# Linear ReLU attention on one core: the last stores cut into 120 and 8 partitions, the first four stores ungated

## The chip, the cores and the metric

One core of a Trainium2 chip runs the kernel. The time is device time in microseconds (us), as the median of several executions. A profile is one execution; its span, from the first to the last instruction, is about 1.8 us shorter than that execution's time.

## The reference

For each of 8 x 12 heads with 512 tokens of 64 numbers, fp32:

```python
Q_feat, K_feat = np.maximum(0, Q), np.maximum(0, K)
KV = np.einsum('bhkd,bhkv->bhdv', K_feat, V)
K_sum = np.sum(K_feat, axis=2)
numerator = np.einsum('bhqd,bhdv->bhqv', Q_feat, KV)
denominator = np.einsum('bhqd,bhd->bhq', Q_feat, K_sum)
return numerator / (denominator[:, :, :, None] + 1e-10)
```

It reads 37.75 MB and writes 12.58 MB, with little arithmetic: the transfers are the work.

## The kernel before

24 groups of four heads. A tile of a group has 128 partitions, each with 16 tokens (4 KB of fp32 in a row of memory). GpSimd issues the loads (they cast to bf16), SyncE the stores. The parts that matter here:

```python
def prep(g): ...      # relu and mask of K, copy of V          (VectorE)
def mm_kv(g):         # 32 small matmuls a group               (TensorE)
    for r in range(R):
        for t in range(2):
            nc.tensor.matmul(ps_kv[g][:, t, 0:D1], kf[g][ts_, r, :, :]..., vo[g % NB][ts_, r, :],
                             start=(r == 0), stop=(r == R - 1), skip_group_check=True)
# ... transposes of Q, output matmuls, normalisation into o_sb ...

def store(g, o_sb):
    if g + DELAY < NG and g % 2 == 0:      # the gate: wait until K of group g + 8 has landed
        nc.sync.dma_start(out=scratch, in_=k_sb[g + DELAY][0:1, 0, :])
    parts = 2 if g >= NG - 4 else 1
    n = R // parts
    for j in range(parts):
        rs = slice(n * j, n * (j + 1))
        nc.sync.dma_start(out=Or[g].rearrange("p (r d) -> p r d", d=D)[:, rs], in_=o_sb[:, rs])

for g in range(NG):   # cut to its order
    mm_kv(g); ...; prep(g + 1); mm_out(g - 1); store(g - 1, norm(g - 1)); transp(g); ...
```

The gate is a load of 128 bytes out of the K tile of eight groups later. SyncE works in order, so it holds back the stores behind it, in favour of the loads. Each transfer has a semaphore, a counter; the trace has 16 raises of it for a transfer that runs on 16 engines, and these are the landing times below.

Of the kernel before, what the change touches and what calls it, by code (L numbers as in the profile page):

```python
# [10 lines left out]
def kernel(  # L11
# [7 lines left out]
    nc = tc.nc  # L19
    B, H, S, D = Q.shape  # L20
    assert D == 64
    P = 128
# [4 lines left out]
    R = S * NHG // P  # L27
    U = R // 2
    NG = NH // NHG
    assert NG * NHG == NH and R == 16  # L30
    DELAY = 8
# [22 lines left out]
    def rview(X):  # L54
        return X.rearrange("b h s d -> (b h s d)").rearrange("(n p f) -> n p f", p=P, f=R * D)

    Qr, Kr, Vr, Or = rview(Q), rview(K), rview(V), rview(out)
# [116 lines left out]



    def store(g, o_sb):
        if g + DELAY < NG and g % 2 == 0:
            nc.sync.dma_start(out=scratch, in_=k_sb[g + DELAY][0:1, 0, :])
        parts = 2 if g >= NG - 4 else 1  # L180
        n = R // parts
        for j in range(parts):
            rs = slice(n * j, n * (j + 1))
            nc.sync.dma_start(out=Or[g].rearrange("p (r d) -> p r d", d=D)[:, rs], in_=o_sb[:, rs])

    zero(0)
    prep(0)
    for g in range(NG):
        mm_kv(g)
        evac_kv(g)  # L190
        if g + 1 < NG:
            if g + 1 < NB:
                zero(g + 1)
            prep(g + 1)
        if g > 0:
            mm_out(g - 1)
            store(g - 1, norm(g - 1))
        transp(g)
        evac_qt(g)
    mm_out(NG - 1)  # L200
    store(NG - 1, norm(NG - 1))


# [28 lines left out]
```

## Time and profile before

| | before |
|---|---|
| time | 130.03 us (129.72 to 130.11, 3 runs) |
| span of the profile | 128.1 us |
| busiest compute engine | DVE, 63% of the span |
| share of the 16 DMA engines | 90% or more in 38 of 40 slices |
| last compute / last store landed | 121.2 us / 126.95 us |

The prediction shows the page's rows. Here is what it doesn't show, the stores and gates in the list of DMA issues of the kernel before. The columns are the tiles, the issuing queue, the count, the size of each and the median us from issue to landing:

```profile
out_dram<-o_sb SPq DMA_DIRECT2D x20, 512.0 KB, 8.8
out_dram<-o_sb SPq DMA_DIRECT2D x8, 256.0 KB, 7.2
scratch<-k_sb SPq DMA_DIRECT2D x8, 0.1 KB, 4.7
```

A store takes 7 to 9 us to land though it moves 0.5 MB: it stands in full queues.

### The profile page before, as it was taken

The numbers are of one execution on the slowest core, as the hardware profiler recorded it, in microseconds if no ns is written. First come the engines' busy times: TensorE is split into PE (matmuls) and PEld (weight loads), VectorE is DVE, ScalarE is ACT, GpSimd is POOL, SyncE is SP. The second block draws the span as 40 slices with busy tenths as digits, with TensorE's granted clock in tenths as the row PEclk, the third lists the DMA queues.
The fourth block names the chain that finished last, engine by engine and source line by source line (L and its number), as shares of the span: only waits on it lengthen the run. The fifth ranks groups of instructions, "written<-read, shape, count | busy, mean of one in ns | idle before, by whom it ended". The sixth has DMA issues, their size and how long they took to land.

```text
span 128.1 us, 4127 instructions
## 1 busy us (share of the span) xinstructions
PE 73.7 (58%) x1728; PEld 54.9 (43%) x1728; DVE 80.3 (63%) x230; ACT 51.0 (40%) x121; POOL 39.4 (31%) x74
## 2 busy tenths in 40 slices
PE   0037864878957818728746855583781874566100
PEld 0036643556644616526535634362460653354100
DVE  1258886798887557748728738456753872886600
ACT  4024774366464433633633452433453363326000
POOL 6905445354535133224133313323331400000000
PEclk9999998555595555555555555555555558757855
DMA  3999999999999999999999999999999999999991
GB/s 109 380 299 212 208 211 209 211 210 209 210 209 260 303 223 241 305 236 232 305 246 211 310 264 211 291 283 209 235 307 242 228 311 246 230 386 411 404 362 67
DMA packets 14673, 32.76 MB, mean 256 GB/s; under 512 B 1856, under 2 KB 1856, under 8 KB 14656
## 3 DMA queue, kind: packets, MB, share of 16 engines
q0 software_dynamic: 9792, 17.83, 74.6%
q1 hardware_dynamic: 4576, 13.63, 28.1%
q10 hardware_dynamic: 288, 1.05, 2.1%
q8 instruction: 13, 0.21, 0.6%
q14 instruction: 4, 0.03, 0.1%
HBM read 37.75 MB, written 12.58 MB: 393 GB/s over the span
## 4 chain that ended last, share of the span: by engine, by line
DMA 79%; POOL 4%; PE 3%; DVE 3%; issue 3%; ACT 2%; POOLq 0%; ACTq 0%
DMA q_sb<-in_Q_dram 41%; DMA v_sb<-in_V_dram 30%; DMA k_sb<-in_K_dram 8%; DVE o_sb L168 2%; ACT qt L143 2%; PE ps_qt L139 1%; POOL q_sb L82 1%; POOL v_sb L78 1%; PE ps_out L154 1%; PE ps_kv L124 1%; POOL k_sb L76 1%; DVE vo L116 1%; DVE rec L167 1%; DVE den L165 0%; POOL ident masks.py:199 0%
## 5 line engine op out<-in xcount | busy, mean ns | idle before, releaser
L124 PE MATMUL ps_kv<-vo,kf 64*128 64x65 bf16 x768 | 24.1, 233 | 32.8 <-DVE vo L116 32.3
L133 ACT CAST kvd<-ps_kv 64x130 bf16<-64x130 f32 x96 | 25.3, 263 | 32.4 <-PE ps_kv L124 30.5
L143 ACT ACTIVATE qt<-ps_qt 128x1024 bf16<-128x1024 bf16 x24 | 24.6, 1024 | 33.4 <-PE ps_qt L139 33.4
L124 PEld LDWEIGHTS <-kf 64*128 64x128 bf16 x768 | 20.5, 122 | 38.3 <-DVE vo L116 30.3
L168 DVE TENSOR_TENSOR o_sb<-ps_out,rec 128x512 f32<-128x512 f32 x48 | 33.2, 691 | 1.7
L154 PE MATMUL ps_out<-kvd,qt 128*32 128x130 bf16 x768 | 28.0, 295 | 10.6 <-DVE o_sb L168 6.5
L114 DVE TENSOR_SCALAR kf<-k_sb,mask 128x1024 bf16<-128x1024 bf16 x44 | 19.4, 483 | 19.3 <-DMA k_sb<-in_K_dram 19.1
L154 PEld LDWEIGHTS <-qt 128*32 128x32 bf16 x768 | 16.9, 123 | 19.3 <-DVE o_sb L168 12.0
L139 PE MATMUL ps_qt<-ident,q_sb 128*128 128x128 bf16 x192 | 23.3, 298 | 2.1 <-DMA q_sb<-in_Q_dram 2.1
L82 POOL DMA_DIRECT2D q_sb<-in_Q_dram x24 | 15.4, 641 | 19.7 <-DMA k_sb<-in_K_dram 16.8
L139 PEld LDWEIGHTS <-q_sb 128*128 128x128 bf16 x192 | 17.4, 135 | 6.6 <-issue 3.8
L78 POOL DMA_DIRECT2D v_sb<-in_V_dram x22 | 11.7, 530 | 25.1 <-DMA q_sb<-in_Q_dram 20.4
L76 POOL DMA_DIRECT2D k_sb<-in_K_dram x22 | 11.9, 541 | 17.8 <-DVE den L165 6.5
L116 DVE COPY vo<-v_sb 128x1024 bf16<-128x1024 bf16 x22 | 9.5, 430 | 10.0 <-DMA v_sb<-in_V_dram 10.0
L167 DVE RECIPROCAL rec<-den 128x8 f32<-128x8 f32 x48 | 9.7, 203 | 1.7
L165 DVE TENSOR_SCALAR den<-ps_out 128x8 f32<-128x8 f32 x48 | 7.5, 156 | 2.0 <-PE ps_out L154 2.0
L114 DVE TENSOR_SCALAR kf<-k_first,mask 128x1024 bf16<-128x1024 f32 x4 | 2.8, 750 | 5.3 <-DMA k_first<-in_K_dram 5.3
L133 ACT ACT_TABLE_LOAD x1 | 1.3, 1283 | 1.7 <-DVE kvd L107 1.7
L116 DVE CAST vo<-v_first 128x1024 bf16<-128x1024 f32 x2 | 1.4, 694 | 0.0
L105 DVE MEMSET mask<- 32x1 f32 x8 | 0.3, 59 | 0.9 <-PEq L216 0.8
L107 DVE MEMSET kvd<- 128x260 f32 x3 | 0.8, 275 | 0.0
masks.py:199 POOL TENSOR_SCALAR_AFFINE_SELECT ident<-ident 128x128 bf16<-128x128 bf16 x1 | 0.3, 287 | 0.1
(6 smaller groups left out, 0.8 us busy)
## 6 DMA issues: line engine op xcount, KB each, us to landing
out_dram<-o_sb SPq DMA_DIRECT2D x20, 512.0 KB, 8.8
q_sb<-in_Q_dram POOLq DMA_DIRECT2D x24, 256.0 KB, 12.5
k_sb<-in_K_dram POOLq DMA_DIRECT2D x22, 256.0 KB, 12.5
v_sb<-in_V_dram POOLq DMA_DIRECT2D x22, 256.0 KB, 12.4
out_dram<-o_sb SPq DMA_DIRECT2D x8, 256.0 KB, 7.2
v_first<-in_V_dram ACTq DMA_DIRECT2D x2, 512.0 KB, 6.7
k_first<-in_K_dram SPq DMA_DIRECT2D x2, 512.0 KB, 6.4
scratch<-k_sb SPq DMA_DIRECT2D x8, 0.1 KB, 4.7
```

The lines of the kernel that those rows point to most:

```text
L76: nc.gpsimd.dma_start(out=k_sb[g].rearrange("p r d -> p (r d)"), in_=Kr[g])
L78: nc.gpsimd.dma_start(out=v_sb[g].rearrange("p r d -> p (r d)"), in_=Vr[g])
L82: nc.gpsimd.dma_start(out=q_sb[g].rearrange("p u f -> p (u f)"), in_=Qr[g])
L114: nc.vector.tensor_scalar(kf[g][:, :, s, :], k_sb[g], scalar1=0.0, scalar2=mask[:, s:s + 1], op0=Alu.max, op1=Alu.mult)
L116: nc.vector.tensor_copy(vo[g % NB][:, :, 0:D], v_sb[g])
L124: nc.tensor.matmul(ps_kv[g][:, t, 0:D1], kf[g][ts_, r, :, :].rearrange("p s d -> p (s d)"), vo[g % NB][ts_, r, :], start=(r == 0), stop=(r ...
L133: nc.scalar.copy(kvd[g % NB][64 * c:64 * c + 64, :, s, c, :], ps_kv[g][64 * s:64 * s + 64, :, 0:D1])
L139: nc.tensor.transpose(ps_qt[g][:, u, :], q_sb[g][:, u, :], ident)
L143: nc.scalar.activation(qt[g].rearrange("p u q -> p (u q)"), ps_qt[g].rearrange("p u q -> p (u q)"), Act.Relu)
L154: nc.tensor.matmul(po[hs, v // 2, (v % 2) * 2 * D1:(v % 2) * 2 * D1 + 2 * D1], qt[g][:, u, hs], kvd[g % NB][:, h // 2, h % 2, :, :], start ...
L167: nc.vector.reciprocal(rec, den)
L168: nc.vector.tensor_tensor(o_sb[:, 8 * j:8 * j + 8].rearrange("p (b r) d -> p b r d", b=2), pv[:, :, :, 0:D], rec.unsqueeze(3).to_broadcast ...
```

## The change

Its intent: one of the 16 DMA engines, number 15, is held to be behind at the end; so the last stores give it nothing. 120 partitions run on the other 15 engines, and the 8 partitions left on the first eight. (This is the rule under (1) in the prediction. Wherever an engine is named below, its number comes from that rule.) With it, the gates of groups 0 and 2 go, and groups 20 and 21 are stored whole.

```diff
     def store(g, o_sb):
-        if g + DELAY < NG and g % 2 == 0:
+        if 4 <= g < NG - DELAY and g % 2 == 0:
             nc.sync.dma_start(out=scratch, in_=k_sb[g + DELAY][0:1, 0, :])
-        parts = 2 if g >= NG - 4 else 1
-        n = R // parts
-        for j in range(parts):
+        last = g >= NG - 2
+        n = R // 2 if last else R
+        for j in range(R // n):
             rs = slice(n * j, n * (j + 1))
-            nc.sync.dma_start(out=Or[g].rearrange("p (r d) -> p r d", d=D)[:, rs], in_=o_sb[:, rs])
+            for ps in (slice(0, 120), slice(120, P)) if last else (slice(0, P),):
+                nc.sync.dma_start(out=Or[g].rearrange("p (r d) -> p r d", d=D)[ps, rs], in_=o_sb[ps, rs])
```

## The prediction

> **What bounds the kernel now.** I read the page first: the DMA row, the chain, the queues; then the waits of SyncE, the busy time by windows, and the landing times that the trace keeps.
>
> ```profile
> DMA  3999999999999999999999999999999999999991
> GB/s 109 380 299 212 208 211 209 211 210 209 210 209 260 303 223 241 305 236 232 305 246 211 310 264 211 291 283 209 235 307 242 228 311 246 230 386 411 404 362 67
> ...
> q0 software_dynamic: 9792, 17.83, 74.6%
> q1 hardware_dynamic: 4576, 13.63, 28.1%
> ...
> q8 instruction: 13, 0.21, 0.6%
> ...
> HBM read 37.75 MB, written 12.58 MB: 393 GB/s over the span
> ...
> DMA 79%; POOL 4%; PE 3%; DVE 3%; issue 3%; ACT 2%; POOLq 0%; ACTq 0%
> ```
>
> The DMA row is 9 in 38 of 40 slices: the transfer engines are full from 3 us to about 124 us, while the busiest compute engine is DVE with 63%. GB/s counts what lands: a load reads fp32 and lands bf16, so 210 there is 420 read. Load stretches (420), mixed stretches and the stores at the end (404 to 411) all move about the same HBM traffic. A store that goes earlier or later only changes the order of work in full queues. What can change the time is idle time at the two ends.
>
> ```profile
> 122.00:124.00 2.00, 0.00 (x0) 0.00 (x0) 0.00 (x0) 0.00 (x0) 0.00 (x0) 0.50 1.04 400
> 124.00:125.00 1.00, 0.00 (x0) 0.00 (x0) 0.00 (x0) 0.00 (x0) 0.00 (x0) 0.50 0.63 244
> 125.00:126.00 1.00, 0.00 (x0) 0.00 (x0) 0.00 (x0) 0.00 (x0) 0.00 (x0) 0.50 0.38 145
> 126.00:127.00 1.00, 0.00 (x0) 0.00 (x0) 0.00 (x0) 0.00 (x0) 0.00 (x0) 0.50 0.11 43
> ```
>
> The last two columns are the DMA engines' share and their GB/s. All compute is over at 121.19 us (end of the last o_sb multiply). Until 124 the engines are full with stores, then they run dry one after the other: a ragged end. The trace keeps 16 landing times for every transfer, one for each DMA engine, without the engine's name. For the last store, after the first at 124.20 us, they come at +0.04, 0.07, 0.31, 0.40, 0.44, 0.79, 0.94, 1.00, 1.41, 1.57, 2.18, 2.52, 2.53, 2.68 and 2.75 us (126.95). Their mean is +1.23. So the whole ragged end is worth at most 2.75 - 1.23 = 1.5 us, 1.2% of the time, even if every engine ended at once. The span ends 1.1 us after the last landing.
>
> ```profile
> SPq L179 <- DMA k_sb<-in_K_dram: 72.3, 8, 33.9
> SPq L179 <- DMA scratch<-k_sb: 20.4, 7, 3.4
> SPq L184 <- DMA out_dram<-o_sb: 6.6, 6, 2.0
> ```
>
> The first line is the gate of the stores: before every even group up to 14, SyncE waits until K of eight groups later has landed (35.5 us for the first, then every 10.2 us). The third matters for the end: a store waits for an older store. The semaphores in the trace show why: SyncE's transfers go round eight semaphores, so each issue waits until the transfer eight before it has landed on all 16 engines. The last six stores were issued at 115.24, 116.86, 118.18, 119.41, 120.64 and 121.85 us, each about 0.06 us after such a landing.
>
> **What the Trainium skill says.** (1) "DMA: Bandwidth & Descriptors", section "Why a DMA increments its semaphore by 16 and not by 1": the number of engines of a transfer is the largest k up to 16 that divides the outer dimension, and on the sync queue these are the lowest-numbered k. So 120 partitions go to engines 0 to 14 with 8 each, and 8 partitions to engines 0 to 7 with one each; engine 15 gets none of the last two groups. The trace before has only transfers cut 16 ways, so it can't test this. (2) Same page, "Latency and other measured facts": engines 7 and 15 are usually slower than the others. This trace does not agree: between 11.5 and 17 us the spread of the 16 landings stays at 0.55 to 0.62 us from load to load, and from 117.8 to 126.95 us it stays at 2.72 to 2.79. An engine with a lower rate would fall back further with every transfer. (3) "Runtime: NRT & Kernel Launch", section "Instruction fetch mechanics": instructions are refilled in 16 KiB blocks over a DMA queue of the sequencer's own. The trace agrees: queue q8 has 13 packets of 16 KB (0.21 MB), of 0.89 to 0.96 us each. After the ones at 16.4, 22.6, 30.6 and 36.7 us one, two, three and then four engines are late by more than 1 us, so these packets fall on different engines and each puts its engine back. The late engines are late by such accidents, not by their nature. (4) "DMA: Bandwidth & Descriptors", "Rules for kernel authors", advises against splitting a transfer over partitions because the parts share the same engines; here the two parts do share engines 0 to 7.
>
> **The change part by part.**
> - *The gate of groups 0 and 2 goes* (4 <= g): two tiny loads of scratch less, and stores 0 to 3 (2.1 MB) leave when their o_sb is ready, from about 16 to 32 us, not from 36.2 and 46.5 us. The engines are full in both stretches, so the loads are put back by the same bytes: 4 stores x 1.25 us (spacing of whole stores on the fastest engine, 114.06 to 115.30) = 5.0 us. Store 4 still waits for K of group 12, which landed at 56.0 us after stores 0 to 3 in either kernel. From there on nothing differs. Worth: 0, give or take 0.3 us by where the instruction packets fall.
> - *Stores of groups 20 and 21 become whole*: four issues become two. On one engine a half store takes 0.65 us (landings 121.63, 122.29, 122.92, 123.56, 124.20), a whole one 1.25, so 2 x (2 x 0.65 - 1.25) = 0.1 us is saved on every engine.
> - *Stores of groups 22 and 23: four become eight.* Engine 15 loses 4 x 0.65 = 2.6 us. Engines 0 to 7 get four packets of 2 KB more, at 0.084 us each (the duration of such a packet in the trace), 0.34 us, and some time for four more completions: I take 0.4. Engines 8 to 14 are as before.
> - *SyncE*: 30 stores and 6 scratch loads in place of 28 and 8, so the same number of issues. But eight transfers back from the end now lie groups 18 to 21: the last four issues wait for stores 18, 19, 20 and 21 whole, that is until about 120.6, 121.8, 123.0 and 124.3 us. The last, of 8 partitions, is then issued 2.5 us later than the last issue of before.
>
> The end is set by the last engine. Of the five late ones (+2.18 to +2.75), engine 15 is at most one. If it is the last, the next ends 0.07 us sooner, and 0.1 from the whole stores: -0.2 us. If the latest one left is among engines 0 to 7, it ends 0.4 - 0.1 = 0.3 us later. With five late engines of 16 it is likely that one of the late ones is among the eight that get more: sum about +0.1 us. Of 130.03 us that makes 130.1.
>
> **The rivals.**
> - *Engine 15 alone is the straggler* (the idea of the change): its removal would give the distance to the next engine. For it speaks the skill's sentence on engine 15; against it that four engines end within 0.23 us of each other. Only if the early stores change where the delays fall could one engine stand out; the gain is then below the 1.5 us of a perfectly even end: 128.6 us at best.
> - *The semaphore wait becomes the end.* Between issue and first packet lies about 1.0 us (the first K load: 0.74 to 1.75 us), so the 8-partition store issued at 124.4 moves from 125.4 and lands around 126.3, still before the late engines' 126.9. The fastest engines run dry for some 0.5 us while the third store from the end (8 partitions of group 23 aside, the second half's 120) waits for store 20, but they have 2.75 us to spare. If landings come 1 us later than I think: 131 us.
> - *The stores in the early stretch starve compute.* DVE needs about 3.7 us for a group there and has few pauses; loads come every 3.75 us. With stores between, loads come slower and compute waits, but the load queue is eight transfers deep and later waits absorb it: 0 us.
> - *Early stores fill idle DMA time*: the row of 9s before 36 us speaks against it; there is none to fill. 0 us.
>
> **Range and chances.** Three runs before spread over 0.4 us. The shift of the late engines is worth -0.2 to +0.3 us, a differently placed instruction packet up to 0.6 us either way at the very end. So 129.5 to 130.7 us should hold eight times in ten. Faster by over 2% would need 2.6 us, more than an even end could give (1.5 us), so 0.01; slower by over 2% would need a wait that I don't see, 0.02.
>
> **What would show each step right or wrong.** The last store's landings should still have a spread of about 2.5 to 3 us with several engines at the end; the half stores of groups 22 and 23 should show 120- and 8-partition forms. SyncE's waits for stores at the store line should grow, with its last issue at about 124.4 us. The first store should leave near 16 us, K of group 12 should land at 56 us as before, and the GB/s row should rise in slices 5 to 10 and fall in 12 to 17. Total DMA time must not change. The prediction would be wrong if one engine stood alone at the end before, if the wait for a semaphore ended last, or if the engines were not truly full in the early stretch.

## The result, and the profile after

The changed kernel took 130.16 us (130.06 to 130.33, 4 runs) against 130.06 (129.72 to 130.11) beside it: ratio 1.0015, interval 0.9994 to 1.0035. A ratio is the mean time of one kernel's fast runs over that of the other's of the same rounds, so it isn't quite the ratio of the medians. Timed again in five rounds it was 130.26 against 129.83 us, ratio 1.0042 (1.0020 to 1.0065). So it is the same at 2%, and slower by about half a microsecond when looked at closely.

The page of the changed kernel, with the rows that answer to those of the prediction:

```profile
DMA  3999999999999999999999999999999999999992
GB/s 119 381 292 209 210 186 270 288 212 286 231 265 211 209 212 209 210 209 219 307 256 209 300 276 209 285 288 212 253 307 225 221 311 249 226 380 410 413 343 92
...
HBM read 37.75 MB, written 12.58 MB: 392 GB/s over the span
...
DMA 79%; DVE 5%; POOL 4%; PE 3%; issue 3%; ACT 1%; POOLq 0%; ACTq 0%
...
out_dram<-o_sb SPq DMA_DIRECT2D x22, 512.0 KB, 8.7
...
out_dram<-o_sb SPq DMA_DIRECT2D x4, 240.0 KB, 6.1
scratch<-k_sb SPq DMA_DIRECT2D x6, 0.1 KB, 4.8
```

The stores have moved forward: the values above the 210 of pure loading stand in slices 7 to 12 now, where those of before began at slice 13. All else is alike, with one new thing: the sixth value, 186, is lower than any in the load stretch of before. The three counts confirm the edit: 22 whole stores, four of 240 KB (120 partitions), six gates.

The end of the changed kernel, by windows (the last two columns again the DMA share and GB/s):

```profile
122.00:124.00 2.00, 0.00 (x0) 0.00 (x0) 0.00 (x0) 0.00 (x0) 0.00 (x0) 0.50 0.96 372
124.00:125.00 1.00, 0.00 (x0) 0.00 (x0) 0.00 (x0) 0.00 (x0) 0.00 (x0) 0.50 0.85 289
125.00:126.00 1.00, 0.00 (x0) 0.00 (x0) 0.00 (x0) 0.00 (x0) 0.00 (x0) 0.50 0.75 275
126.00:127.00 1.00, 0.00 (x0) 0.00 (x0) 0.00 (x0) 0.00 (x0) 0.00 (x0) 0.50 0.25 94
```

Before 124 us the engines have small pauses now (372, not 400 GB/s), after it more is left to do (289 and 275, not 244 and 145). This is the fast engines waiting for the next store; the slow ones aren't touched by it. The landing times show it engine by engine. In each row the trace's times for one store, one for each engine that carries it, in order of time:

```
before, last store (16 engines):
 124.20 124.24 124.27 124.51 124.60 124.64 125.00 125.14 125.20 125.61 125.77 126.38 126.72 126.73 126.88 126.95
after, whole store of group 21 (16 engines), us after its first at 121.95:
 0 0.23 0.23 0.42 0.45 0.48 0.94 1.28 1.33 1.54 1.64 1.75 2.62 2.64 2.65 2.97
after, next store, 120 partitions of group 22 (15 engines), us after its first at 122.61:
 0 0.21 0.22 0.42 0.43      0.95 1.27 1.33 1.54 1.65 1.73 2.60 2.61 2.64 2.96
after, last store of 120 partitions (15 engines):
 125.82 125.87 125.92 126.00 126.01 126.06 126.07 126.08 126.10 126.16 126.53 127.13 127.14 127.16 127.48
```

Rows two and three name engine 15, the one that the rule leaves out. They are the same engines in the same order, but one is missing in the third row, and it is one of those at 0.42 to 0.48: **engine 15 was 2.5 us ahead of the last.** The four late ones, at 2.6 us and more, are all still there. The part of 8 partitions of that same half landed between 122.83 and 124.55 on engines 0 to 7, while the four late landings of the 120-partition part came at 125.21 to 125.57; so the late four are among engines 8 to 14. The change took work from an engine that had time, and gave it to eight that had time too. In the last row eleven engines, which had been spread over 1.75 us, land within 0.7: they ran dry and waited for a store that was issued late. The last four did not wait: they still come within 0.35 us of each other, now 1.3 to 1.7 us after the first.

SyncE's waits after the change (who waited for what: us in total, times, longest us):

```profile
SPq L180 <- DMA k_sb<-in_K_dram: 52.3, 6, 24.8
SPq L186 <- DVE o_sb L168: 31.5, 6, 14.2
SPq L180 <- DMA scratch<-k_sb: 14.9, 5, 3.5
...
SPq L186 <- DMA out_dram<-o_sb: 2.6, 4, 1.0
```

Six gates are left of eight. The first stores now wait for their own data (DVE, 31.5 us). SyncE's wait for older stores has become less and not more.

After the early stores everything is late: K of group 12 landed at 56.40 us (before: 55.98), the whole store of group 21 at 124.92 (before, its second half: 124.38). From there to the last landing, it took 2.56 us after (124.92 to 127.48) and 2.57 before (124.38 to 126.95). So in these two profiles the half microsecond of the last landing does not come from the cut of the last stores at all.

### The profile page after: what moved, and what is told of

It reads as the page before. It is cut to its first block, busy times and chain, and to the rows that moved or that the text cites. A ratio compares the mean times of both kernels' runs of the same rounds, so it can differ in the third digit from the quotient of the medians.

```text
span 128.5 us, 4124 instructions
## 1 busy us (share of the span) xinstructions
PE 74.1 (58%) x1728; PEld 55.1 (43%) x1728; DVE 80.2 (62%) x230; ACT 51.1 (40%) x121; POOL 39.7 (31%) x74
## 4 chain that ended last, share of the span: by engine, by line
DMA 79%; DVE 5%; POOL 4%; PE 3%; issue 3%; ACT 1%; POOLq 0%; ACTq 0%
DMA q_sb<-in_Q_dram 39%; DMA v_sb<-in_V_dram 32%; DMA k_sb<-in_K_dram 9%; DVE o_sb L168 3%; PE ps_out L154 1%; POOL q_sb L82 1%; POOL v_sb L78 1%; DVE rec L167 1%; PE ps_kv L124 1%; POOL k_sb L76 1%; PE ps_qt L139 1%; ACT qt L143 1%; DVE vo L116 1%; DVE den L165 1%; POOL ident masks.py:199 0%
## 5 line engine op out<-in xcount | busy, mean ns | idle before, releaser
L124 PE MATMUL ps_kv<-vo,kf 64*128 64x65 bf16 x768 | 24.6, 236 | 33.7 <-DVE vo L116 33.4
```

The source lines that it names most:

```text
L124: nc.tensor.matmul(ps_kv[g][:, t, 0:D1], kf[g][ts_, r, :, :].rearrange("p s d -> p (s d)"), vo[g % NB][ts_, r, :], start=(r == 0), stop=(r ...
```

## The experiments

The first question was which part of the change costs, the second which engine is late, and the third why.

**1. The cut of the last stores alone.** The changed store with the gate of before:

```diff
-        if 4 <= g < NG - DELAY and g % 2 == 0:
+        if g + DELAY < NG and g % 2 == 0:
```

> The gate of the kernel before is kept; only the stores of the last four groups are cut as in the change. Theory A (engine 15 is not among the late engines, the end belongs to others): same as before within 0.4 us, last landing about 0.1 us earlier to 0.3 us later. Rival B (the split gains and the earlier first stores give the gain back): faster than before by 0.5 us or more. Rival C (the wait for the eighth transfer back costs): slower by 0.5 us or more, and no late engine is busy at the end.

130.41 us against 129.87, ratio 1.0044 (1.0026 to 1.0061): slower by half a microsecond. But the last landing, at 127.08 us, was only 0.13 us later than before, as theory A said; its time, the same within 0.4 us, was missed. Rival C had the time right, but the late engines landed last here too (126.64 to 127.08 us). Engine 15, missing in the first 15-engine store, was this time at 0.73 us of a spread of 3.15. The rest of the loss lies behind the last landing. SyncE's closing waits started, after it, at

```
127.09 127.16 127.22 127.28 127.34 127.40 127.46 127.52   then the end of waiting at 127.59
```

and in the kernel before a single one, at 126.97, with the end of waiting at 127.03. At the end SyncE waits for its eight semaphores one by one in a fixed order. This kernel has two transfers of SyncE more than the kernel before, so that the latest store's semaphore is first in that order, not last, and all others are paid behind it. From the last landing to the end of the span it took 1.53 us here and 1.11 before. Experiment 4 tests this by itself. The whole change has 40 transfers on these semaphores as the kernel before has, so it does not have that loss.

**2. The gate alone.** The other half: the changed gate, with the stores cut as before.

```diff
-        if g + DELAY < NG and g % 2 == 0:
+        if 4 <= g < NG - DELAY and g % 2 == 0:
```

> Only the gate of groups 0 and 2 goes; the last stores are cut as before. Theory A: within 0.3 us of before, since the engines are full in either order. Rival B: slower by 0.3 to 0.6 us (in the changed kernel's profile everything from K of group 12 on was 0.4 us later than before).

130.49 us against 129.87, ratio 1.0043 (1.0023 to 1.0063), last landing 127.59 us. Rival B's size was right: leaving early costs the first four stores half a microsecond, which the prediction's "only changes the order of work in full queues" had ruled out. The place can be seen in windows of one microsecond. The kernel before:

```profile
18.00:19.00 1.00, 0.57 (x27) 0.33 (x23) 0.93 (x4) 0.58 (x3) 0.00 (x0) 1.00 1.10 205
19.00:20.00 1.00, 0.66 (x28) 0.37 (x28) 0.60 (x1) 0.48 (x2) 0.53 (x1) 1.00 1.16 217
```

The changed kernel:

```profile
18.00:19.00 1.00, 0.50 (x19) 0.24 (x12) 0.93 (x4) 0.71 (x4) 0.00 (x0) 1.00 1.17 150
19.00:20.00 1.00, 0.75 (x28) 0.47 (x29) 0.55 (x1) 0.43 (x2) 0.53 (x1) 1.00 1.02 156
```

Gate alone:

```profile
18.00:19.00 1.00, 0.44 (x28) 0.45 (x30) 0.86 (x4) 0.25 (x1) 0.53 (x1) 1.00 1.12 154
19.00:20.00 1.00, 0.57 (x32) 0.45 (x24) 0.93 (x4) 0.61 (x3) 0.53 (x1) 0.89 1.11 154
```

Both kernels with early stores lose a quarter of the rate for two microseconds, about 2 x (1 - 153/211) = 0.55 us (an estimate from the means of these windows). The DMA share stays above 1, so "busy" doesn't show it: the load packets themselves take up to 0.48 us there (0.17 as a rule). The first store was issued at 15.88 us, and its first data packet started at 19.83: the dip lies between the two.

**3. Which engines are late?** A probe on the kernel before: the last two of 16 rows of the stores of groups 16 to 21 are cut by partitions.

```diff
+        Ov = Or[g].rearrange("p (r d) -> p r d", d=D)
+        cut = {NG - 8: 120, NG - 7: 126, NG - 6: 117, NG - 5: 104, NG - 4: 108, NG - 3: 110}.get(g)
+        if cut:
+            nc.sync.dma_start(out=Ov[:, 0:R - 2], in_=o_sb[:, 0:R - 2])
+            for ps in (slice(0, cut), slice(cut, P)):
+                nc.sync.dma_start(out=Ov[ps, R - 2:], in_=o_sb[ps, R - 2:])
+            return
```

> A probe on the kernel before: of the stores of groups 16 to 21 the last two rows go in two parts of 120/8, 126/2, 117/11, 104/24, 108/20 and 110/18 partitions, which by the skill's rule run on 15, 14, 13, 13, 12 and 11 engines, lowest-numbered first. Comparing their landing times with those of the 16-way store before them shows how late engines 15, 14, 13, 12 and 11 are. Theory A: engine 15 is not the last; taking 15 away leaves four or five late landings (over 2 us after the first). Rival B: the latest landing goes with engine 15. Time within 1 us of before.

131.01 us, 1.1 us over the kernel before and so just outside the expected 1 us (the many small stores let engines run dry). The rows, in us after the first landing of each:

```
group 16, 16 engines: 0 0.05 0.15 0.30 0.33 0.39 0.52 1.11 1.13 1.59 1.61 2.12 2.38 2.40 2.62 2.92
group 16, 120 rows, 15 engines: 0 0.07 0.16 0.34 0.34 0.38 1.11 1.14 1.59 1.61 2.13 2.38 2.43 2.63 2.90
group 16, 8 rows, 8 engines: 0 0.10 0.34 0.36 0.38 1.11 1.17 2.15
group 18, 16 engines: ... 1.32 1.51 2.08 2.33 2.34 2.59 2.77
group 18, 117 rows, 13 engines: ... 1.54 1.77 1.79 2.02 2.20
```

Engine 15 is the one at 0.52. The latest landings stay when engines 13, 14 and 15 are all left out (five late ones in either row of group 18), and only one of the late five is among engines 0 to 7. So the late four are engines 8 to 12. Leaving out the top engine can't reach them. From group 19 on the engines were nearly level, and the finer cuts told nothing more.

**4. Two more transfers of SyncE**, and nothing else, to move the last store's semaphore away from the last place:

```diff
+    more = [consts.tile([1, D], bf16, name=f"more{i}") for i in range(2)]
...
+        if g == 4:
+            for i in range(2):
+                nc.sync.dma_start(out=more[i], in_=k_sb[g][0:1, 0, :])
```

> The kernel before with two more 128-byte loads of SyncE at group 4, so that the last store has the second of the eight semaphores and not the last. Theory A (SyncE's final waits go through the eight semaphores in a fixed order, 0.06 us each, so those that follow the last landing are paid): last landing as before within 0.2 us, 0.3 to 0.45 us later end: ratio about 1.003. Rival B (the last landing alone counts): within 0.1 us of before.

130.56 us against 129.83, ratio 1.0053 (1.0037 to 1.0069), more than expected. Last landing 127.14 us (0.2 later than before), and behind it closing waits at 127.16, 127.25, 127.33, 127.40, 127.47, 127.94 and 128.02, with the end of waiting at 128.09: 0.95 us after the last landing, 0.08 before. To the end of the span it took 1.78 us from the last landing, and 1.11 before, so 0.67 us of the difference stayed. The order of the closing waits is shown as a cost. A pause of 0.47 us within them, which made it larger than I had worked out, is not explained.

**5. Fewer instructions.** One row block of 16 in the K-V product, which makes the result wrong on purpose (a relative error of 3.8) and leaves every transfer as it is:

```diff
-        for r in range(R):
+        for r in range(1):
...
-                    start=(r == 0), stop=(r == R - 1), skip_group_check=True)
+                    start=(r == 0), stop=True, skip_group_check=True)
```

> Result wrong on purpose: the K-V product takes one row block of 16, so PE has about 2000 instructions and not 3458; all transfers are as before. Theory A (each 16 KB packet of instructions puts one DMA engine back): 7 or 8 packets on q8 in place of 13, the spread of the last store's landings falls from 2.75 to 2 us or less, and the time by 0.5 to 1.3 us. Rival B (late engines are slow by nature): spread and time as before within 0.3 us.

128.62 us against 129.87, ratio 0.9903 (0.9885 to 0.9920): 1.25 us faster, though in the kernel before all compute is over 5.8 us before the last landing. The queues of this run:

```profile
q8 instruction: 8, 0.13, 0.4%
```

8 packets of instructions in place of 13. The last store's spread fell from 2.75 to 1.72 us and the last landing from 126.95 to 125.77. Its windows at the end, to be held against those of before in the prediction:

```profile
124.00:125.00 1.00, 0.00 (x0) 0.00 (x0) 0.00 (x0) 0.00 (x0) 0.00 (x0) 1.00 0.59 227
125.00:126.00 1.00, 0.00 (x0) 0.00 (x0) 0.00 (x0) 0.00 (x0) 0.00 (x0) 1.00 0.07 25
```

The granted clock was 1.0 here and 0.62 before, so this run alone leaves the clock as a rival.

**6. More instructions.** 18 matmuls of one column a group, whose result the next matmul overwrites, for 22 groups; the output is right.

```diff
+        for _ in range(18 if g < NG - 2 else 0):
+            nc.tensor.matmul(ps_kv[g][:, 0, 0:1], kf[g][0:64, 0, :, :]..., vo[g % NB][0:64, 0, 0:1],
+                             start=True, stop=True, skip_group_check=True)
```

> Result as the reference. 18 one-column matmuls a group for 22 groups, overwritten by what follows: about 790 more PE instructions, hence 16 packets of instructions and not 13. Theory A: last landing 0.2 to 1.0 us later (3 x 0.94 us over 16 engines is 0.18 as a mean, 0.94 if one hits the latest engine), time up by as much. Rival B (instruction packets do not matter, what changed in the run with fewer of them was the PE clock): time as before within 0.15 us.

A miss: 130.01 us against 129.83, ratio 1.0007 (0.9989 to 1.0024), last landing 126.93, though there were 16 packets:

```profile
q8 instruction: 16, 0.26, 0.7%
```

The landings told why. The last store's came in two groups: eight engines at 0 to 1.09 us after the first, and eight at 2.23 to 2.89. With 8 packets it had been seven up to 0.62 and nine from 1.11 to 1.72; with 13, eleven up to 1.57 and five from 2.18. That looks like eight engines that take the packets in turn: 8 packets are one each, 13 are two for five of them, and 16 are two for all. (It is no exact count: with 8 packets nine engines were behind, not eight.) Then 16 needn't be later than 13, but more than 16 would be.

**7. Eighteen packets**, to test that: 28 matmuls in place of 18.

> 28 one-column matmuls a group in place of the 18 of the run before: some 4690 PE instructions, 18 packets of instructions. Refined theory A2 (these packets go in turn to the same eight DMA engines, so with 8 packets each of the eight is hit once, with 13 five of them twice, with 16 all of them twice): with 18 two engines are hit a third time and stand alone at the end, the last landing 0.6 to 1.2 us later than before, time up by as much, landings in groups of about 8, 6 and 2. Rival B2 (they fall anywhere, or only the PE clock mattered): last landing and time within 0.3 us of the run with 16 packets.

131.08 us against 129.93, ratio 1.0083 (1.0064 to 1.0102); last landing 128.24, 1.29 us later than before and just over the expected 1.2.

```profile
q8 instruction: 18, 0.29, 0.8%
```

```profile
127.00:128.00 1.00, 0.00 (x0) 0.00 (x0) 0.00 (x0) 0.00 (x0) 0.00 (x0) 0.50 0.09 35
```

Here the engines are still at work after 127 us (share 0.09: less than two of 16). The last store but one landed, after its first, at 0 to 1.23 us (eight engines), 1.93 to 2.84 (six), and 3.58 and 3.95 (two). Eight, six and two was the expected pattern. The granted clock was 0.65, near that of before, and one of the other runs of this kernel had 0.953 and still took 131.02 us, so it isn't the clock. A second rival is late compute: the last multiply ended at 122.49 us (before: 121.19), and the last store was issued at 123.28 us (before: 121.85). But the two latest engines landed the last store 0.64 and 0.65 us after the one before it, the usual time of half a store, so they never waited for it.

The trace of the kernel before shows the turn within one run. As its first eight packets pass, stretches of loads alone show 1, 2, 3, 4, 5, 6, 7 and 8 engines that land over 1 us after the first. After packets 9 to 13 there are 1, 2, 3, 4 and 5 that land over 2 us after it (the loads of K that began to land at 78.45, 88.60, 98.77 and 107.72 us, and the last store). **So what makes an engine late is how many packets of instructions it was given**, as far as counts can show it: the trace doesn't say which eight engines take the packets.

**8. The dip with the small load kept.** Groups 0 and 2 keep their small transfer, but out of a K that has landed long before:

```diff
-            nc.sync.dma_start(out=scratch, in_=k_sb[g + DELAY][0:1, 0, :])
+            ahead = g + DELAY if g >= 4 else g + 2
+            nc.sync.dma_start(out=scratch, in_=k_sb[ahead][0:1, 0, :])
```

> As the gate-only kernel, but groups 0 and 2 keep their small load of scratch, from the K of two groups later, which has landed by then, so stores 0 to 3 still leave early. Theory A (the dip of the transfer rate at 17.5 to 20 us comes with the first large store on a SyncE queue that has been idle): the small load takes the cold start, the dip goes, and the time is within 0.2 us of before. Rival B (an early store as such costs): dip and 0.4 to 0.7 us stay.

130.39 us against 129.83, ratio 1.0040 (1.0026 to 1.0053), and at 18 to 20 us it moved 135 and 162 GB/s. The idea of a cold queue fell.

**9. The first store at 25 us**, by a gate on K of five groups later (`g + 5` in place of `g + 2` above):

> As the gate-only kernel, but groups 0 and 2 wait for K of five groups later (about 24.7 and 34 us), so store 0 leaves near 25 us and not at 16. If the dip of the transfer rate (17.5 to 20 us) belongs to the first store, it moves to about 26 to 29 us and the time stays 0.4 to 0.7 us over before. If it belongs to a large store in flight at that time of the load stream only, it is gone and the time is within 0.25 us of before.

130.15 us against 129.93, ratio 1.0015 (0.9999 to 1.0032). Neither expectation held fully: the rate kept its 210 at 18 to 20 us, and a smaller dip came with the store, whose data started at 29 us:

```profile
28.00:29.00 1.00, 0.98 (x21) 0.78 (x22) 0.88 (x2) 0.25 (x1) 0.74 (x1) 0.50 1.20 189
```

So the dip goes with the first store, just ahead of its data. It costs 0.5 us for a store at 16 us, perhaps 0.2 at 25 us (the interval just includes no difference), and no dip can be seen at 36 us, where the kernel before has its first store. Why there is a dip, and why the early one costs more, was not settled.

**10. The changed kernel again**, on the chip of runs 4, 6 and 8:

> The changed kernel once more, on the same chip as the next runs. Reading of the first four runs: the early stores cost 0.5 us (gate only: 0.56), the split itself costs the last engine nothing (with the split alone the last landing came 0.13 us later, and the other 0.4 us were the order of the final semaphore waits, which the change does not have). So before plus 0.2 to 0.6 us. If the parts simply added up (split only 0.54 plus gate only 0.56) it would be 1.1 us over before.

130.26 us against 129.83, ratio 1.0042 (1.0020 to 1.0065), last landing 127.30. The parts alone cost 0.44% and 0.43%, and together 0.42% and not 0.87%, since the cut alone paid for the order of the semaphores, and in the whole change the two gates less restore that order.

No version here beats both kernels. The one that was faster computes less. A program with at most 8 packets of instructions and the right result would need some 1,200 to 1,400 of the 3,508 TensorE instructions fewer (an estimate: experiment 5 took out 1,440 for five packets less, experiment 7 put in 1,232 for five more); I saw no such rewriting that leaves the stores in rows of 4 KB.

## Why the prediction was right

- *The bound.* Right: full DMA engines to 124 us, compute over at 121 us, and a ragged end that could give at most 1.5 us. This made a gain of 2% impossible before anything else was known. The run whose end was least ragged (experiment 5) gained 1.25 us.
- *The gate: "Worth: 0, give or take 0.3 us".* This term was mis-sized. The first store left at 15.88 us as predicted, K of group 12 landed within 0.4 us of the predicted 56 us, and the rate fell in the stretch that I named; it rose a slice later than I said, after the dip. But early stores cost 0.5 us (experiments 2 and 8). The step that failed is that full engines move the same bytes per microsecond in any order; at 18 to 20 us they were full by the page and a quarter slower.
- *Whole stores of groups 20 and 21: 0.1 us saved.* Right: from the first landing of group 19's store to the first of the end of group 21's took 2.59 us before (119.04 to 121.63) and 2.50 with whole stores (118.91 to 121.41 in experiment 1).
- *Engine 15 is at most one of the late ones.* Right, and more than that: it was an early one (0.45 of 2.97 us), so nothing was gained by relieving it, not even the 0.07 us I allowed.
- *Engines 0 to 7 pay 0.4 us.* Right in size, as their landings from one half of group 22 to the next were some 0.73 us apart where 0.64 was usual, four times 0.09. But "it is likely that one of the late ones is among the eight" was wrong: the latest four were all in 8 to 14, and the end paid none of it (2.56 against 2.57 us).
- *The wait for the eighth transfer back.* Right: the last four of these issues, predicted for about 120.6, 121.8, 123.0 and 124.3 us, came at 121.25, 122.44, 123.73 and 124.94, each just after the store named had landed (121.19, 122.42, 123.66 and 124.92). The 8-partition store landed at 126.72, before the last engine of the other part. That SyncE's waits for stores would grow was wrong: 2.6 us after, 6.6 before, as fewer issues are left that wait so.
- *The rivals.* The straggler rival fell with the missing engine of the 15-engine stores. The rival "Early stores fill idle DMA time" fell; the true effect had the other sign.
- *The sum.* +0.1 us predicted; 0.1 us in the first rounds, 0.43 in the later ones by the medians, inside the range both times. The part that is beyond +0.1 is the dip, less what the last stores did not cost. So the sum is near by some luck: the gate cost 0.5 us where I had 0, the last stores cost nothing where I had allowed up to +0.3, and the two errors partly cancel.

## What to carry to other kernels

Where the DMA engines are full to the end, read the landing times engine by engine before you rebalance anything: a transfer that leaves one engine out names that engine by the time that goes missing. A late engine needn't be a slow one: here it was delayed by packets of the program's own instructions, so instructions on an idle-looking engine can cost time at the end. And a transfer more or less can shift which semaphore the last store carries, worth 0.4 to 0.7 us in the two runs that tried it; compare the last landing and the end separately.

## What the Trainium skill lacked or had wrong

- "DMA: Bandwidth & Descriptors", section "Latency and other measured facts", calls engines 7 and 15 usually slower. Here engine 15 was among the early ones in three kernels: at 0.45 of 2.97 us, 0.73 of 3.15 and 0.52 of 2.92. Engine 7 was not told apart. (The page calls its reason a guess and ties it to transfers that GpSimd issues, as most loads here are.)
- "Runtime: NRT & Kernel Launch", section "Instruction fetch mechanics", has the 16 KiB blocks, which agrees with the packets, and calls the cost of crossing a block mostly hidden. It lacks what a block costs where the DMA engines are full, and so does every other page: 0.88 to 0.97 us each as a rule on the engine that takes it, which by the counts is one of some eight of the 16, in turn; the time went from 128.62 us (8 packets) over 129.8 to 130.0 (13 and 16) to 131.08 (18).
- "DMA: Bandwidth & Descriptors", section "Why a DMA increments its semaphore by 16 and not by 1": its rule for the number of engines held. The 120-partition stores have 15 landings and the 8-partition stores 8 in these traces (one more raise of the semaphore within 1 us of the issue, before any data, is not counted). Nothing was wrong there; that these are the lowest-numbered engines, no run here shows.
- No page has the closing waits: eight semaphores one after the other, 0.06 to 0.09 us each, which went on for 0.5 us after the last landing in one run and 0.95 in another (there with a pause of 0.47), against 0.08 where the last store has the last semaphore.
- No page has the dip of a load stream before the first store's data: 150 and 156 GB/s in place of 205 and 217 for two microseconds at 16 us, and less for a later store.
